# A hybrid decoder block on one core: filler products of both attentions in another order, the bias table written from another queue, four output tiles finished at full width

## The chip, the cores and the metric

The kernel runs on one core of one Trainium2 chip. A core has TensorE (PE: matmuls; its weight loads are shown as PEld), VectorE (DVE), ScalarE (ACT), GpSimd (POOL) and SyncE (SP, which here only issues DMAs). Each engine works through its own instructions in order and waits for the others by semaphores. DMAs are issued from an engine's queue; in this kernel SP issues nearly all of them. The metric is the device time of one execution in microseconds (us), as a median over runs.

## The reference

One layer for 512 tokens of width 1024 and 256 memory tokens, all in float32. Two kinds of heads read the same normed x; then come cross-attention and an MLP:

```python
h = rms_norm(x, norm_mix[l])
qa, ka, va, qg, kg, vg, glr, rg = jnp.split(h @ w_in[l], offsets, axis=-1)
o_a = moba_attention(qa, ka, va, rp_table)
log_a = jax.nn.log_sigmoid(glr @ w_gate_up[l] + b_gate[l]) / G_GATE_NORM
o_g = gla_chunked(qg, kg, vg, log_a)
o_g = rms_norm(o_g, g_norm[l]).reshape(B, T, G_WIDTH) * jax.nn.silu(rg)
x = x + jnp.concatenate([o_a, o_g], axis=-1) @ w_out[l]
...
return rms_norm(x, norm_final)
```

`o_a` has 8 heads of 64, causal, with a bias by relative position; `o_g` has 4 heads. Left out are cross-attention (xq, kx, vx, xo) and the MLP with its squared ReLU, each added to x. With two blocks of 256 tokens the block-sparse attention sees all earlier tokens, so it is causal softmax attention with a bias by distance.

## The kernel before

**Precision and products.** Each float32 operand is split into two float16 parts, high and low, by an ACT copy and a DVE subtraction (`split`, L276 to L278; for weights L115 and L116, into tiles whl). A product is three matmuls: high by high, high by low, low by high. `gemm_steps` (L225) gives one such step of three matmuls for each 128 rows of the contraction; a tile of 512 tokens takes 8 steps, 24 matmuls of 512 columns.

**Order on PE.** PE's order is the order in which the code is written; the other engines' instructions are put in order by a scheduler, and a wait on one of them holds all that stands behind it there. To keep PE busy while another engine prepares the next thing, the code has a list of fillers (`Fill`, L252): generators of product steps, of which `fill(n)` runs the next n, `fill.until(k)` runs until k generators are left and `fill.drain()` runs all. Which product is in the list where (L744 to L746, L895, L907) and the numbers of the calls set PE's order.

**GLA stage (L744 to L787).** `Gla(pr)` makes the gates of two of the four heads: product z, then on ACT Abs, Exp, Ln (tile e) and on DVE two scans. `prep_fine` makes qF and kF (ACT exponents L577, L578; DVE L579, L580), which `small` multiplies into psL (L610); `prep_level` makes qz and kz, whose tiles POOL sets to zero (L590, L591), for the next products into psL. Fillers here are vg (values of the GLA heads), qk(0) and qk(1) (queries and keys of head pairs 0 and 1), and the memory's keys and values xk and xv.

**Memory squares.** `mem_steps` (L474) loads the memory tokens, splits them and sums their squares: four ACT squares (sqm), added on POOL into accm (L487, L491). The tiles sqm have two buffers, one of which was bvec's.

**Bias table.** bvec (8 heads by 384 distances) goes to DRAM as bscr1 (L724), and from there 128 times, each copy one element further, into the table bscr (L727): 1024 rows. Both writes are issued from ACT's queue. `load_bias` (L735) reads a pair's bias from it through SP and spreads one column on POOL (bq, L741).

**Attention stage (L895 to L921).** For each pair of heads i, `score` runs four query tiles (3, 2, 1, 0): s = q k (L810), maximum, exponent and sum, then P in two parts (pq, L838, L839). `trans` transposes P by DMA (L845), `attn_out` multiplies it by v (o, L857). A score needs the pair's qks, the split result of qk(i): eviction (L415), ACT split (L277), DVE split (L278). Fillers are va, qk(2), rg(1), qk(3), rg(2), rg(3); rg is the gate of the GLA output, with a chain of its own on ACT and DVE (L527 to L542) that ends in a part of mix, the input of the output projection.

**Output projection (L863 to L941).** Four of its eight tiles (NPRE) are begun early, over the parts of mix that are there (`early_steps`). `residual_steps` then finishes tile by tile for one half of the tokens (256), adds x (xr, L883) and sums the squares (`SumSq`: ACT L316, POOL L326, L327). While PE works on the second half, `normed` computes the first half's norm: total on PE (L332), ACT L284 to L286, DVE L287 and L289 (wout), then eight times a product (ynout, L299) and a split into act2, which the first xq products read.

Of the kernel before, what the change touches and what calls it, by code (L numbers as in the profile page):

```python
# [39 lines left out]
def hybrid_block_kernel(  # L40
# [163 lines left out]
    for n in range(8):  # L204
        W.add(("xv", n), w_xv[n])
    W.add(("tt", 8), w_tt[8])
    for n in range(4):
        W.add(("va", n), w_vv[n])
    for n in (2, 6, 9, 3, 7, 10, 11):
        W.add(("tt", n), w_tt[n])  # L210
    for nm, ap in (("out", w_out), ("xq", w_xq), ("xo", w_xo)):
        for n in range(8):
# [261 lines left out]
    def mem_steps():  # L474
        memf = [p1.tile([P, 2, M], F32, tag="va", bufs=4, name=f"memf{j}") for j in range(4)]
        accm = pst.tile([P, 512], F32, tag="acc", bufs=1, name="accm")
        for j in range(4):
            nc.sync.dma_start(memf[j], mem_t[:, 2 * j:2 * j + 2, :])
        for j in range(4):
            mf = memf[j].rearrange("p n t -> p (n t)")  # L480
            for k in (2 * j, 2 * j + 1):
                mk = memf[j][:, k % 2, :]
                ACT.activation(actm[k][:, 0, :], mk, AF.Copy, scale=gmem[:, k:k + 1])
                DVE.scalar_tensor_tensor(actm[k][:, 1, :], mk, gmem[:, k:k + 1], actm[k][:, 0, :], op0=ALU.mult, op1=ALU.subtract)
            if j == 0:
                ACT.activation(accm, mf, AF.Square)
                POOL.tensor_scalar(accm, accm, 512 * EPS / P, None, op0=ALU.add)  # L487
            else:
                sq = pst.tile([P, 512], F32, tag="sq", bufs=2, name=f"sqm{j}")
                ACT.activation(sq, mf, AF.Square)  # L490
                POOL.tensor_tensor(accm, accm, sq, op=ALU.add)  # L491
            yield from ()
        mem_acc.append(accm)

    mem_acc = []

# [48 lines left out]
    class Gla:  # L545
# [175 lines left out]
    bvec = pst.tile([P, 512], F32, tag="sq", bufs=2, name="bvec")[0:8, :NDIST]  # L721
    DVE.tensor_copy(bvec, psb[0:8, 0:NDIST])
    bscr1 = pdr.tile([8, NDIST], F32, name="bscr1")
    nc.scalar.dma_start(bscr1, bvec)  # L724
    bscr = pdr.tile([8, P, T], F32, name="bscr")

    nc.scalar.dma_start(  # L727
        bass.AP(tensor=bscr.tensor, offset=bscr.offset, ap=[[P * T, 8], [T + 1, P], [1, NDIST]]),
        bass.AP(tensor=bscr1.tensor, offset=bscr1.offset, ap=[[NDIST, 8], [0, P], [1, NDIST]]),
    )  # L730
# [10 lines left out]
            POOL.tensor_copy(bq[:, :256], bq[:, 256:257].to_broadcast([P, 256]))  # L741
            bias[p].append(bq)

    fill.add(*[vg_steps(t) for t in range(4)], qk_steps(0), mem_steps(), qk_steps(1), memsum_steps())  # L744
    fill.add(xk_steps(0), xk_steps(1), memrow_steps(), *[xk_steps(n) for n in range(2, 8)])
    fill.add(*[xv_steps(c, t) for c in range(2) for t in range(2)])  # L746
    gl = []
    for pr in range(2):
        fill(8 if pr == 0 else 4)
        gl.append(Gla(pr))  # L750
        if pr == 0:
            pw_ = sbank("wxt")
            for t in range(4):
                PE.transpose(pw_[:, t * P:t * P + P], wx[:, t * P:t * P + P], ident)
            DVE.tensor_scalar(wxt, pw_.rearrange("p (n t) -> p n t", t=P)[:, :, 0], SA * IX, None, op0=ALU.mult)
    for pr in range(2):
        if pr == 1:
            load_bias(0)
        G = gl[pr]
        a = G.prep_fine()  # L760
        fill(20 if pr == 0 else 6)
        G.banks()
        G.small(0, a)
        for i, s in enumerate((8, 16)):
# [107 lines left out]

    def residual_steps(nm, act, hf, ssq):
        c0 = hf * HT
        for n in range(8):
            if nm == "out" and n < NPRE:
                ps = early[n][:, c0:c0 + HT]
                yield from gemm_steps(ps, (nm, n), act, c0, c0 + HT, (2, 3), start=False, skip_group_check=True)
            else:
                ps = gbank(f"{nm}{n}_{hf}")[:, :HT]  # L880
                yield from gemm_steps(ps, (nm, n), act, c0, c0 + HT)
            xs = xr[n][:, c0:c0 + HT]
            DVE.scalar_tensor_tensor(xs, ps, IS, xs, op0=ALU.mult, op1=ALU.add)  # L883
            ssq.add(xs)

    xr = [None] * 8

# [527 lines left out]
```

## Time and profile before

| what | value |
| --- | --- |
| median of three runs | 715.57 us (715.09 to 715.87) |
| the profiled execution | 715.83 us, span 714.0 us |
| mean granted clock of TensorE | 0.983 |
| PE busy | 682.5 us, 96% of the span |
| DVE busy | 551.7 us, 77% |
| ACT busy | 417.0 us, 58% |
| POOL busy | 73.6 us, 10% |

The span is the time from the first to the last instruction in one profiled execution; the execution took 1.8 us more. In a timeline, a bracket such as `[6.79 <-DVE kF L580]` is the time that the engine had stood idle before that instruction, and the instruction that ended the wait. [...] `SPq` and `ACTq` are instructions that issue DMAs.

### The profile page before, as it was taken

How to read it: one execution, taken by the hardware profiler on the slowest of the kernel's cores; microseconds unless marked ns; L12 is line 12 of the kernel's file. 1: busy time of each engine (PE TensorE's matmuls, PEld its weight loads, DVE VectorE, ACT ScalarE, POOL GpSimd, SP SyncE). 2: the span in 40 equal slices, each digit the busy share in tenths (PEclk: the TensorE clock that was granted, in tenths of full speed). 3: DMA queues.
4: the chain of work that ended last, by engine and by line, in shares of the span. 5: the costliest groups of instructions: out<-in, count | busy, mean ns of one | idle time of the engine just before them, and what ended most of it. 6: DMA issues, size and time to landing. Idle time of an engine off the chain costs nothing.

```text
span 714.0 us, 13411 instructions
## 1 busy us (share of the span) xinstructions
PE 682.5 (96%) x5352; PEld 469.4 (66%) x5352; DVE 551.7 (77%) x987; ACT 417.0 (58%) x800; POOL 73.6 (10%) x90
## 2 busy tenths in 40 slices
PE   8996999999898997999999999999999999999995
PEld 3443486544343486888888854468888866488884
DVE  6957969768986638656639899889878889999825
ACT  8646465668775436355536666545444766665533
POOL 4013000000000044000124100000000000003211
PEclk9998999999998999899999999999999999999999
DMA  8860643443826604236404231203343352314003
GB/s 310 277 231 16 211 142 118 163 151 66 258 90 171 185 1 148 89 62 176 105 16 143 95 118 60 88 31 120 118 129 110 123 167 64 118 54 136 20 1 119
DMA packets 57059, 85.68 MB, mean 120 GB/s; under 512 B 32123, under 2 KB 37540, under 8 KB 56996
## 3 DMA queue, kind: packets, MB, share of 16 engines
q1 hardware_dynamic: 55948, 83.24, 37.2%
q10 hardware_dynamic: 1048, 1.59, 0.6%
q8 instruction: 42, 0.69, 0.4%
q14 instruction: 21, 0.17, 0.1%
HBM read 75.36 MB, written 3.68 MB: 111 GB/s over the span
## 4 chain that ended last, share of the span: by engine, by line
PE 56%; DVE 7%; ACT 3%; issue 2%; POOL 1%; DVEq 0%; ACTq 0%; POOLq 0%
PE up L233 6%; PE up L231 6%; PE up L232 6%; PE a L1186 4%; PE a L1187 4%; PE a L1188 4%; PE xq L232 2%; PE xq L233 2%; PE xq L231 2%; PE c L1187 2%; PE c L1186 2%; PE c L1188 2%; DVE whl L116 1%; PE xo L233 1%; PE xo L232 1%
## 5 line engine op out<-in xcount | busy, mean ns | idle before, releaser
L116 DVE SCALAR_TENSOR_TENSOR whl<-wst,whl 128x1024 f16<-128x1024 f32 (+1 forms) x165 | 195.5, 1191 | 27.1 <-ACT whl L115 26.5
L115 ACT ACTIVATE whl<-wst 128x1024 f16<-128x1024 f32 (+1 forms) x165 | 166.2, 1014 | 44.0 <-PE a L1188 7.8
L233 PEld LDWEIGHTS <-whl 128*128 128x128 f16 x744 | 73.5, 99 | 44.0 <-issue 6.1
L231 PEld LDWEIGHTS <-whl 128*128 128x128 f16 x744 | 73.4, 99 | 39.8 <-issue 4.5
L232 PEld LDWEIGHTS <-whl 128*128 128x128 f16 x744 | 73.4, 99 | 38.4 <-issue 3.8
L231 PE MATMUL up<-act,whl 128*128 128x512 f16 (+1 forms) x224 | 78.1, 349 | 0.0
L232 PE MATMUL up<-act,whl 128*128 128x512 f16 (+1 forms) x224 | 78.1, 349 | 0.0
L233 PE MATMUL up<-act,whl 128*128 128x512 f16 (+1 forms) x224 | 78.1, 349 | 0.0
L1186 PE MATMUL a<-t,whl 128*128 128x256 f16 x192 | 52.3, 273 | 1.1 <-ACT v L1203 1.1
L1187 PE MATMUL a<-t,whl 128*128 128x256 f16 x192 | 52.3, 273 | 0.0
L1188 PE MATMUL a<-t,whl 128*128 128x256 f16 x192 | 52.3, 273 | 0.0
L1187 PEld LDWEIGHTS <-whl 128*128 128x128 f16 x456 | 44.6, 98 | 6.9 <-issue 1.5
L1186 PEld LDWEIGHTS <-whl 128*128 128x128 f16 x456 | 44.6, 98 | 5.2
L1188 PEld LDWEIGHTS <-whl 128*128 128x128 f16 x456 | 44.6, 98 | 4.9
L232 PE MATMUL xq<-act,whl 128*128 128x256 f16 x128 | 36.0, 281 | 3.3 <-DVE act L278 3.3
L231 PE MATMUL xq<-act,whl 128*128 128x256 f16 x128 | 35.9, 281 | 0.9 <-ACT act L277 0.9
L233 PE MATMUL xq<-act,whl 128*128 128x256 f16 x128 | 36.0, 281 | 0.0
L233 PE MATMUL xo<-ox,whl 128*128 128x256 f16 x128 | 34.9, 273 | 0.0
L232 PE MATMUL xo<-ox,whl 128*128 128x256 f16 x128 | 34.9, 273 | 0.0
L231 PE MATMUL xo<-ox,whl 128*128 128x256 f16 x128 | 34.9, 273 | 0.0
L277 ACT ACTIVATE t<-hs 128x512 f16<-128x512 f32 x32 | 19.8, 624 | 23.9 <-DVE hs L1068 23.8
L232 PE MATMUL out<-mix,whl 128*128 128x256 f16 (+1 forms) x104 | 30.9, 297 | 0.1
(334 smaller groups left out, 1642.8 us busy)
## 6 DMA issues: line engine op xcount, KB each, us to landing
wst<-in_w_up SPq DMA_DIRECT2D x32, 512.0 KB, 3.6
wst<-in_w_down SPq DMA_DIRECT2D x32, 512.0 KB, 3.7
wst<-in_w_tt SPq DMA_DIRECT2D x12, 512.0 KB, 4.6
wst<-in_w_vv SPq DMA_DIRECT2D x8, 512.0 KB, 3.5
wst<-in_w_xk SPq DMA_DIRECT2D x8, 512.0 KB, 5.7
wst<-in_w_xv SPq DMA_DIRECT2D x8, 512.0 KB, 3.5
wst<-in_w_out SPq DMA_DIRECT2D x8, 512.0 KB, 4.8
wst<-in_w_xq SPq DMA_DIRECT2D x8, 512.0 KB, 3.6
```

The lines of the kernel that those rows point to most:

```text
L115: ACT.activation(wt[:, 0, c], stg[:, c], AF.Copy, scale=SW)
L116: DVE.scalar_tensor_tensor(wt[:, 1, c], stg[:, c], SW, wt[:, 0, c], op0=ALU.mult, op1=ALU.subtract)
L231: PE.matmul(ps, wt[:, 0, kt, :], a[:, 0, c0:c1], start=st, stop=False, **kw)
L232: PE.matmul(ps, wt[:, 0, kt, :], a[:, 1, c0:c1], start=False, stop=False, **kw)
L233: PE.matmul(ps, wt[:, 1, kt, :], a[:, 0, c0:c1], start=False, stop=sp, **kw)
L277: ACT.activation(dst_h, src, AF.Copy, scale=scale)
L1186: PE.matmul(ps, w[:, 0, kt, :], b[:, 0, c], start=st, stop=False, skip_group_check=not start)
L1187: PE.matmul(ps, w[:, 0, kt, :], b[:, 1, c], start=False, stop=False, skip_group_check=not start)
L1188: PE.matmul(ps, w[:, 1, kt, :], b[:, 0, c], start=False, stop=sp, skip_group_check=not start)
```

## The change

It has four parts.

- **GLA stage.** Both `Gla` objects are made at one place, after seven filler steps; the steps after the first `prep_fine` are 25 instead of 20, those after the second 8 instead of 6. `mem_steps` now runs inside `qk_steps(1)`, one of its four pieces every four steps.
- **Bias table.** Both writes are issued from POOL's queue.
- **Attention stage.** The fillers stand in the order qk(2), va, qk(3), rg(1), rg(2), rg(3), with the weights in a matching order, and the counts between scores and the places of `attn_out` change.
- **Output projection.** The four early tiles are finished for all 512 tokens within the first half; the second half has the other four tiles alone.

```diff
-    for n in (2, 6, 9, 3, 7, 10, 11):
+    for n in (3, 7, 9, 10, 11):
...
-        for j in range(4):
+        for j, _ in enumerate(qk_steps(1)):
+            yield
+            if j % 4 or j > 12:
+                continue
+            j //= 4
             mf = memf[j].rearrange("p n t -> p (n t)")
...
-    nc.scalar.dma_start(bscr1, bvec)
+    nc.gpsimd.dma_start(bscr1, bvec)
...
-    nc.scalar.dma_start(
+    nc.gpsimd.dma_start(
         bass.AP(tensor=bscr.tensor, offset=bscr.offset, ap=[[P * T, 8], [T + 1, P], [1, NDIST]]),
...
-    fill.add(*[vg_steps(t) for t in range(4)], qk_steps(0), mem_steps(), qk_steps(1), memsum_steps())
+    fill.add(*[vg_steps(t) for t in range(4)], qk_steps(0), mem_steps(), memsum_steps())
...
-        fill(8 if pr == 0 else 4)
-        gl.append(Gla(pr))
...
+    fill(7)
+    gl = [Gla(0), Gla(1)]
...
-        fill(20 if pr == 0 else 6)
+        fill(25 if pr == 0 else 8)
...
+        if nm == "out":
+            ns = range(NPRE, 8)
+            if hf == 0:
+                for n in range(NPRE):
+                    yield from gemm_steps(early[n], (nm, n), act, 0, T, (2, 3), start=False, skip_group_check=True)
+                    DVE.scalar_tensor_tensor(xr[n], early[n], IS, xr[n], op0=ALU.mult, op1=ALU.add)
+                    for i in range(2):
+                        ssq[i].add(xr[n][:, i * HT:i * HT + HT])
...
-    fill.add(*[va_steps(t) for t in range(4)], qk_steps(2), rg_steps(1), qk_steps(3), rg_steps(2), rg_steps(3))
+    fill.add(qk_steps(2), *[va_steps(t) for t in range(4)], qk_steps(3), *[rg_steps(h) for h in (1, 2, 3)])
...
-            fill.until({2: 4, 3: 2}[i])
+            fill.until({2: 4, 3: 3}[i])
...
-                fill(5 if i < 3 else 3)
+                fill((5, 6, 5, 3)[i])
...
-            if 1 <= i < 4 and g == 3:
-                fill.until(5)
-                attn_out(pairs.pop(i - 1))
+        if 1 <= i < 4:
+            if i == 1:
+                fill.until(4)
+            fill((0, 4, 0, 4)[i])
+            attn_out(pairs.pop(i - 1))
         if i < 4:
             pairs[i].trans()
-            fill(4)
+            fill((4, 0, 0, 0)[i])
```

What stands in a row on the engines that wait, at three places. First POOL from the memory's first square on, before:

```order
L487 TENSOR_SCALAR accm_807<-accm_807 128x512
L741 COPY bq0_1191<-bq0_1191 128x256
L741 COPY bq1_1194<-bq1_1194 128x256
L491 TENSOR_TENSOR accm_807<-accm_807,sqm1_822 128x512
L491 TENSOR_TENSOR accm_807<-accm_807,sqm2_829 128x512
L491 TENSOR_TENSOR accm_807<-accm_807,sqm3_836 128x512
L590 MEMSET qz8_0_629 128x32x8
L591 MEMSET kz8_0_630 128x32x8
```

and after:

```order
L730 DMA bscr1_413<-bvec_411 8x384
L493 TENSOR_SCALAR accm_807<-accm_807 128x512
L733 DMA bscr_415<-bscr1_413 8x128x384
L596 MEMSET qz8_0_629 128x32x8
L597 MEMSET kz8_0_630 128x32x8
L596 MEMSET qz16_0_686 128x16x16
L597 MEMSET kz16_0_687 128x16x16
L497 TENSOR_TENSOR accm_807<-accm_807,sqm1_881 128x512
L497 TENSOR_TENSOR accm_807<-accm_807,sqm2_911 128x512
L497 TENSOR_TENSOR accm_807<-accm_807,sqm3_936 128x512
L747 COPY bq0_1191<-bq0_1191 128x256
L747 COPY bq1_1194<-bq1_1194 128x256
```

The adds into accm have moved from behind the two bias copies to ahead of them, and the two table writes and the memsets of qz and kz stand ahead of both.

Second, DVE at the first score of pair 3, before (L814 ISA is the score's addition of bias with its maximum, p3_3_0 the first of pair 3; qkf7 and qks7 are pair 3's keys; whl is a weight split):

```order
L415 SCALAR_TENSOR_TENSOR qkf7_2409<-qk7_2347,wx_124 128x512
L116 SCALAR_TENSOR_TENSOR whl48_2815<-wst48_2814,whl48_2815 128x1024
L278 SCALAR_TENSOR_TENSOR qks7_2408<-qkf7_2409,qks7_2408 128x512
L814 ISA p3_3_0_2431,sm4_3_2422<-s3_3_0_2423,bq6_2171 128x512
L814 ISA sm4_3_2422 128x1
L814 ISA p3_3_1_2433,sm4_3_2422<-s3_3_1_2424,bq7_2174 128x512
```

and after, DVE at the eviction of pair 3's keys, which stands further ahead, at pair 2's last score tile (p2_0_0) and behind the pieces of pair 2's tiles 3 and 2 (pq2):

```order
L842 SCALAR_TENSOR_TENSOR pq2_0_2261<-p2_2_0_2252,sm4_2_2196,pq2_0_2261 128x3x128
L842 SCALAR_TENSOR_TENSOR pq2_1_2262<-p2_2_1_2254,sm4_2_2196,pq2_1_2262 128x3x128
L818 TENSOR_SCALAR sm4_2_2196<-sm4_2_2196 128x2
L417 SCALAR_TENSOR_TENSOR qkf7_2309<-qk7_2232,wx_124 128x512
L817 ISA p2_0_0_2339,sm4_2_2196<-s2_0_0_2331,bq4_1965 128x128
```

The keys' eviction now stands ahead of pair 2's last score tile. DVE at pair 3's scores after the change (rgsq1, rgnw1 belong to rg(1); p3_2 is pair 3's second score tile):

```order
L544 SCALAR_TENSOR_TENSOR rgsq1_2369<-rgsq1_2369,rgnw1_2370 128x512
L818 TENSOR_SCALAR sm4_3_2422<-sm4_3_2422 128x2
L817 ISA p3_2_0_2455,sm4_3_2422<-s3_2_0_2447,bq6_2197 128x384
L817 ISA sm4_3_2422 128x1
L545 SCALAR_TENSOR_TENSOR rgnw1_2370<-rgsq1_2369,rgnw1_2370 128x512
L817 ISA p3_2_1_2457,sm4_3_2422<-s3_2_1_2448,bq7_2200 128x384
```

rg(1)'s chain, which ended before pair 3's keys, runs between pair 3's scores.

Third, DVE at the norm behind the output projection, before (xr is the addition to x, wout0 the norm's factor of the first half, ynout0_0 the first normed tile):

```order
L883 SCALAR_TENSOR_TENSOR xr3_2625<-out3_2689,xr3_2625 128x256
L116 SCALAR_TENSOR_TENSOR whl52_3164<-wst52_3163,whl52_3164 128x1024
L116 SCALAR_TENSOR_TENSOR whl53_3196<-wst53_3195,whl53_3196 128x1024
L883 SCALAR_TENSOR_TENSOR xr4_2627<-out4_1_2990,xr4_2627 128x256
L287 SCALAR_TENSOR_TENSOR wout0_3107<-ssqout0_2981,wout0_3107 128x256
L116 SCALAR_TENSOR_TENSOR whl54_3230<-wst54_3229,whl54_3230 128x1024
L289 SCALAR_TENSOR_TENSOR wout0_3107<-wout0_3107,yout0_3106 128x256
L116 SCALAR_TENSOR_TENSOR whl55_3262<-wst55_3261,whl55_3262 128x1024
L883 SCALAR_TENSOR_TENSOR xr5_2629<-out5_1_3019,xr5_2629 128x256
L299 SCALAR_TENSOR_TENSOR ynout0_0_3113<-xr0_2619,gneg_87,wout0_3107 128x256
```

and after:

```order
L891 SCALAR_TENSOR_TENSOR xr4_2627<-out4_1_2960,xr4_2627 128x256
L116 SCALAR_TENSOR_TENSOR whl55_3234<-wst55_3233,whl55_3234 128x1024
L289 SCALAR_TENSOR_TENSOR wout0_3079<-ssqout0_2982,wout0_3079 128x256
L291 SCALAR_TENSOR_TENSOR wout0_3079<-wout0_3079,yout0_3078 128x256
L891 SCALAR_TENSOR_TENSOR xr5_2629<-out5_1_2991,xr5_2629 128x256
L301 SCALAR_TENSOR_TENSOR ynout0_0_3085<-xr0_2619,gneg_87,wout0_3079 128x256
L301 SCALAR_TENSOR_TENSOR ynout0_1_3089<-xr1_2621,gneg_87,wout0_3079 128x256
L301 SCALAR_TENSOR_TENSOR ynout0_2_3093<-xr2_2623,gneg_87,wout0_3079 128x256
L280 SCALAR_TENSOR_TENSOR act2_0_2748<-ynout0_0_3085,act2_0_2748 128x256
```

Two of the four weight splits ahead of ynout0_0 stood between the parts of the norm's chain; in the new piece one stands ahead of wout0, and none between it and ynout0_0.

## Rows read from the trace of the kernel before

**Rows 1.** Page, parts 1 (busy) and 5 (count, busy us, mean ns, idle).
```profile
PE 682.5 (96%) x5352; PEld 469.4 (66%) x5352; DVE 551.7 (77%) x987; ACT 417.0 (58%) x800; POOL 73.6 (10%) x90
...
L116 DVE SCALAR_TENSOR_TENSOR whl<-wst,whl 128x1024 f16<-128x1024 f32 (+1 forms) x165 | 195.5, 1191 | 27.1 <-ACT whl L115 26.5
```

**Rows 2.** Windows at the table's write and place 1; the first row names columns.
```profile
core 0: us, PE busy (x) PEld busy (x) DVE busy (x) ACT busy (x) POOL busy (x), PEclk, DMA share, GB/s
40.00:54.40 14.40, 14.40 (x67) 6.49 (x65) 6.53 (x11) 6.56 (x13) 0.07 (x1) 1.00 0.48 170
61.50:65.40 3.90, 3.84 (x72) 1.86 (x73) 3.90 (x8) 3.88 (x8) 0.56 (x2) 0.50 0.00 0
```

**Rows 3.** PE's timeline, first GLA products: start us, us, operation, idle before.
```profile
54.39 0.38 PE L248 MATMUL vg<-whl,act 128*128 128x512 f16 x1
...
61.56 0.89 PE L610 MATMUL psL<-qF,kF 64*32 64x32 f32 x64 [6.79 <-DVE kF L580]
...
111.55 0.75 PE L610 MATMUL psL<-qF,kF 64*32 64x32 f32 x64 [1.38 <-DVE kF L580]
```

**Rows 4.** Timelines of ACT, SP and POOL, 38 to 59 us.
```profile
38.99 0.73 ACTq L727 DMA_DIRECT2D bscr<-bscr  x1
...
53.65 0.81 SPq L740 DMA_DIRECT2D bq<-bscr  x2
...
55.85 0.84 POOL L741 COPY bq<-bq 128x256 f32<-128x256 f32 x2 [15.78 <-DMA bq<-bscr]
56.66 4.30 POOL L491 TENSOR_TENSOR accm<-accm,sqm 128x512 f32<-128x512 f32 x3
...
57.95 0.63 ACT L490 ACTIVATE sqm<-memf 128x512 f32<-128x512 f32 x1 [4.61 <-POOL accm L491]
```

**Rows 5.** PE's timeline at the first scores of pairs 2 and 3.
```profile
192.28 0.39 PE L810 MATMUL s<-qks,qks 64*128 64x512 f16 x2 [1.69 <-ACT qks L277]
193.35 0.61 PE L810 MATMUL s<-qks,qks 64*128 64x512 f16 x4 [0.68 <-DVE qks L278]
...
215.75 0.61 PE L810 MATMUL s<-qks,qks 64*128 64x512 f16 x2 [2.67 <-ACT qks L277]
216.83 1.03 PE L810 MATMUL s<-qks,qks 64*128 64x512 f16 x4 [0.47 <-DVE qks L278]
```

**Rows 6.** Windows from pair 3's first score to o(3), columns as in rows 2.
```profile
217.20:222.60 5.40, 5.40 (x19) 1.47 (x15) 1.48 (x5) 1.52 (x4) 0.00 (x0) 0.51 0.94 245
222.60:238.50 15.90, 15.90 (x99) 7.33 (x98) 13.14 (x40) 12.41 (x30) 0.00 (x0) 1.00 0.50 167
238.50:245.20 6.70, 6.63 (x32) 2.75 (x31) 5.00 (x8) 1.98 (x3) 0.00 (x0) 1.00 1.06 237
```

**Rows 7.** DVE's timeline, end of rg(1), pair 2's last pieces.
```profile
211.16 0.68 DVE L278 SCALAR_TENSOR_TENSOR mix<-rgx,mix 128x512 f16<-128x512 f32 x1
...
213.04 1.40 DVE L839 SCALAR_TENSOR_TENSOR pq<-p,sm,pq 128x256 f16<-128x256 f32 x4
```

**Rows 8.** DVE's and PE's timeline at o(3).
```profile
243.93 0.69 DVE L278 SCALAR_TENSOR_TENSOR mix<-rgx,mix 128x512 f16<-128x512 f32 x1 [0.69 <-ACT mix L277]
...
245.20 1.82 PE L857 MATMUL o<-pT,vas 128*64 128x512 f16 x24
```

**Rows 9.** Timelines of PE, ACT and DVE along the norm behind the out projection.
```profile
266.24 0.60 PE L332 MATMUL ssqout<-accout,ones 128*128 128x256 f32 x2
...
269.69 0.42 ACT L316 ACTIVATE sqout<-xr 128x256 f32<-128x256 f32 x1 [1.54 <-POOL accout L327]
...
276.67 1.74 DVE L299 SCALAR_TENSOR_TENSOR ynout<-xr,gneg,wout 128x256 f32<-128x256 f32 x3
...
284.60 0.75 DVE L278 SCALAR_TENSOR_TENSOR act<-ynout,act 128x256 f16<-128x256 f32 x2
```

**Rows 10.** Windows at the first xq product, columns as in rows 2.
```profile
277.60:285.00 7.40, 3.25 (x20) 1.82 (x19) 7.40 (x17) 5.36 (x11) 3.15 (x3) 0.92 0.27 80
285.00:290.60 5.60, 5.54 (x25) 3.88 (x25) 3.04 (x5) 0.60 (x2) 2.06 (x1) 0.50 0.71 221
```

More of the change, by code (lines that the diff above doesn't have):

```diff
@@ L206, in hybrid_block_kernel @@
     W.add(("tt", 8), w_tt[8])
+    for n in (2, 6):
+        W.add(("tt", n), w_tt[n])
     for n in range(4):
         W.add(("va", n), w_vv[n])
-    for n in (2, 6, 9, 3, 7, 10, 11):
+    for n in (3, 7, 9, 10, 11):
         W.add(("tt", n), w_tt[n])
@@ L491, in mem_steps @@
                 POOL.tensor_tensor(accm, accm, sq, op=ALU.add)
-            yield from ()
-        mem_acc.append(accm)
+            if j == 3:
+                mem_acc.append(accm)
     mem_acc = []
@@ L742, in load_bias @@
             bias[p].append(bq)
-    fill.add(*[vg_steps(t) for t in range(4)], qk_steps(0), mem_steps(), qk_steps(1), memsum_steps())
+    fill.add(*[vg_steps(t) for t in range(4)], qk_steps(0), mem_steps(), memsum_steps())
     fill.add(xk_steps(0), xk_steps(1), memrow_steps(), *[xk_steps(n) for n in range(2, 8)])
     fill.add(*[xv_steps(c, t) for c in range(2) for t in range(2)])
-    gl = []
-    for pr in range(2):
-        fill(8 if pr == 0 else 4)
-        gl.append(Gla(pr))
[L751 to L755, printed above, removed]
+    fill(7)
+    gl = [Gla(0), Gla(1)]
+    pw_ = sbank("wxt")
+    for t in range(4):
+        PE.transpose(pw_[:, t * P:t * P + P], wx[:, t * P:t * P + P], ident)
+    DVE.tensor_scalar(wxt, pw_.rearrange("p (n t) -> p n t", t=P)[:, :, 0], SA * IX, None, op0=ALU.mult)
     for pr in range(2):
@@ L874, in residual_steps @@
         c0 = hf * HT
[L875 to L881, printed above, removed]
+        ns = range(8)
+        if nm == "out":
[6 more added lines that the diff above has]
+                        ssq[i].add(xr[n][:, i * HT:i * HT + HT])
+        for n in ns:
+            ps = gbank(f"{nm}{n}_{hf}")[:, :HT]
+            yield from gemm_steps(ps, (nm, n), act, c0, c0 + HT)
             xs = xr[n][:, c0:c0 + HT]
             DVE.scalar_tensor_tensor(xs, ps, IS, xs, op0=ALU.mult, op1=ALU.add)
-            ssq.add(xs)
+            ssq[hf].add(xs)
     xr = [None] * 8
@@ L906, in hybrid_block_kernel @@
             load_xr()
-            fill.add(early_steps(), residual_steps("out", mix, 0, ssq[0]))
+            fill.add(early_steps(), residual_steps("out", mix, 0, ssq))
         for g in range(4):
@@ L936, in hybrid_block_kernel @@
     fill.drain()
-    fill.add(residual_steps("out", mix, 1, ssq[1]))
+    fill.add(residual_steps("out", mix, 1, ssq))
     fill(7)
@@ L1026, in hybrid_block_kernel @@
     ssq = sums("xo", *HALVES)
-    fill.add(residual_steps("xo", ox, 0, ssq[0]))
+    fill.add(residual_steps("xo", ox, 0, ssq))
     xattn(1)
     fill.drain()
-    fill.add(residual_steps("xo", ox, 1, ssq[1]))
+    fill.add(residual_steps("xo", ox, 1, ssq))
     fill(7)
```

## The prediction

> **What bounds the kernel.** The page comes first: PE is busy 682.5 of 714.0 us, DVE 551.7, ACT 417.0 [rows 1]. So the time is TensorE's stream, and only two things can shorten it: fewer matmul columns, or less time in which PE waits or runs at its lower clock. The change takes 24 weight loads and 24 matmuls away but no columns: 48 products of 256 columns become 24 of 512. [...] What is left is PE's idle time. I went along PE's own timeline for idle brackets, and through windows around them for the granted clock. Five places hold nearly all of it:
>
> 1. First GLA product. PE starts the last matmul of its vg tile at 54.39 and psL at 61.56 [rows 3]: 7.0 lost. [...] Together 8.5.
> 2. The same product of the second GLA pair: 1.38 idle at 111.55 [rows 3].
> 3. Pair 2's first score: 1.69 + 0.68 idle [rows 5], 2.4, at full clock.
> 4. Pair 3's first score: 2.67 + 0.47 idle [rows 5], 3.1, and then 5.4 us at clock 0.51 [rows 6], which costs half of them, 2.6: 5.7.
> 5. The first xq product, behind the out projection: 20 matmuls of 256 columns in 7.4 us, where 2.2 would do, and then 5.54 us busy at clock 0.50 [rows 10]: 5.2 + 2.8 = 8.0.
>
> Together 26.0 us.
>
> **Place 1: the table and the memory squares.** The chain is read backwards. psL waits for DVE's kF [rows 3], that for ACT's exponents, and those stand in ACT's queue behind a square (L490) at 57.95 that waited 4.61 us for POOL's accm. POOL began these three adds (4.30 us) only at 56.66, behind two bq copies at 55.85, for whose data it had sat 15.78 us [rows 4]. bq is read from the table that ACT's queue writes at 38.99. After the change POOL does the adds first and the copies last, and mem's squares are spread over qk_steps(1), ahead of their use. That takes the wait off this chain. What replaces it: ACT's square of the third piece now waits until POOL's small write, bscr1, has landed, since it takes bvec's buffer, and Gla(0)'s Abs, Exp and Ln and the two exponents of qF and kF are queued behind it on ACT. In before the same landing was over by 38.99, when ACT's second write went out. Counting from there with Gla's operations at 0.4 to 0.7 us each, two scans at 1.2, and the vg copy and a whl split among them (1.19 [rows 1]), I estimate kF at 51.5. PE needs it at 54.5, so there are 3 us of slack; below that the cost is nothing, above it 1 for 1. Moving z by three matmuls costs 0.1 at most. Gain 8.4.
>
> The two POOL writes have no row: no DMA goes out on POOL in before. The nearest rows are ACT's: the large write took 0.73 us to issue, which is the lower bound. For the upper one I let POOL be held from there until SP's bq loads go, 39.7 to 53.65, 13.9 us [rows 4]. Queued behind the write are four memsets, and the first user of these is the second psL product, at 54.5 + 0.7 + 12 x 0.213 = 57.8. Neither end reaches PE. I take no cost, being nearest to the 0.73; from 57.8 on it is 1 for 1. On SP the bq loads wait for the table with weight loads behind them; they now stand behind ten weight tiles instead of five, so the tiles that PE needs next are ahead of them.
>
> Where that write goes out DVE is busy 6.53 of 14.40 us [rows 2]. [...]
>
> **Place 2.** fill(8) for fill(6) puts two more steps, six matmuls of 512 columns or as many of 256 twice over, 1.3 us, ahead of the second psL. Gain 1.3.
>
> **Places 3 and 4: the scores.** qk(2) now stands before the va products and qk(3) before rg(1): pair 2's keys are finished 32 steps ahead of its first score and pair 3's eight, where there was one step. Eight steps are 24 x 0.213 = 5.1 us, against the 3.1 that PE waited for the eviction and the splits [rows 5]. Both losses go: 2.4 + 5.7 = 8.1.
>
> What is late next is the tail of pair 3. rg(1) used to be through DVE by 211.16 [rows 7], before pair 3's scores. Now its seven DVE operations (up to 0.68 each, 4.8) fall among them, with pair 2's last four pieces (1.40) and o(1)'s split (0.69): 6.9 us more. From 217.2 to 245.2 DVE is busy 1.48 + 13.14 + 5.00 = 19.6 of 28.0 us [rows 6]; of its 8.4 idle, 2.6 were PE's half clock and go, 5.8 stay. The tail has little slack: the last mix was split from 243.93 for 0.69, so to 244.6, and o(3) goes at 245.20 [rows 8]; pair 3's transposes land at about the same time. 6.9 into 5.8 is 1.1 over if every gap can be filled, and 0 if the stall's end helps ACT as much; 3.2 if three waits of DVE for ACT like the 0.69 at 243.93 [rows 8] stay; 8 if all of it and a split of 1.19 land behind the last product. I take 3.5, nearest to the wait that is a row. Idleness of 3.1 was followed by the half clock at place 4, of 2.4 was not at place 3, so I add 1.5, about half of a stretch like place 4's. 5.0 lost at o(3); attention nets 3.1.
>
> **Place 5: out.** Four out tiles are finished at full width in the first half, so its second half has 32 steps, not 40. From the total of the squares (266.24 [rows 9], after seven of these steps) to xq there are 25 steps x 3 x 0.107 = 8.0 us where there were 10.6: 2.6 less cover. Against it, the chain from that total to the first ynout took until 276.67, 10.4 us; of that 1.54 was ACT's wait for POOL [rows 9], and three whl splits of 1.19 [rows 1] stood in DVE's way. In the new order the slots of out0 to out3 come free 2.6 us earlier and their followers' splits go ahead: one split stands before wout and none between it and the first ynout, where there were two on either side; the squares of the four full tiles are added long before. 10.4 - 1.5 - 3.6 = 5.3. The eight pairs of ynout and act then took 276.67 to 284.60 + 0.75, 8.7 [rows 9]; with one split fewer among them about 7.9. So the last act stands 13.2 after the total, and PE wants it at 8.0 + 7 x 0.321 = 10.3. 2.9 us of idleness remain, in pieces, so I count no half clock. Gain 8.0 - 2.9 = 5.1. Bounds: all hidden, 8.0; only the cover lost, -2.6.
>
> **The sum.** 8.4 + 1.3 + 3.1 + 5.1 = 17.9. From the first xq product on the order is the same. The profiled execution took 715.83 (span 714.0 and 1.8 around it), 0.26 above the median of 715.57: 715.83 - 17.9 - 0.26 = 697.7. I forecast **697.5 us**, rounded.
>
> **Rivals.**
> - A: pair 3's tail fits, and the norm's last act comes in time. DVE's gaps before 222.6 are waits for PE at half clock, which speaks for it. 697.5 - 5.0 = 692.5, with the norm hidden too 689.6.
> - B: the tail gives attention's gain back: 8 idle and 2.7 at half clock at o(3) for the 5.0. The little slack of before speaks for it. 703.2.
> - C: the norm chain keeps its length and only loses cover: 8.0 + 2.6 for 2.9. Against it, the splits do stand elsewhere in the order. 705.2.
> [...]
> - E, slower: POOL is held by the 1024 rows of the table write itself. PE loses 1 for 1 past 57.8; to lose 17.9 and 1.4 more it must be held to 77.1, 37.4 us for one write, 50 times ACT's issue. From there on the time is above 717.
> - F: the losses only move (place 1's to the second psL, 3 and 4's to o(2) and o(3), 5 as in C): near 715.5.
>
> **Chances.** Forecast 0.44, A 0.22, B 0.11, C 0.09, D 0.07, E 0.05, F 0.02. The range leaves out E, F and little besides: 690 to 706. Faster by over 0.2% (about what a measurement of this kernel can tell from no change): all but E and F, 0.93; within 0.2%: 0.02; slower: 0.05.
>
> **What will show it.** Right: no idle bracket over 1 us at psL near 54.5, POOL's adds ahead of its copies and its DMA issues short; none ahead of the first scores of pairs 2 and 3; one of 0 to 5 us near o(3), released by DVE's mix or the transposes; some 3 us of waits for act at xq, with clock 1.00 after. Wrong: PE waiting between 55 and 65 for a memset or for ACT's exponents (D, E), clock 0.50 after o(3) (B), waits of 5 us and more at xq (C).

## The result, and the profile after

The changed kernel took 707.69 us (706.36 to 710.12, four runs), the kernel before 715.72 (715.09 to 717.06): a ratio of 0.9889, 95% interval 0.9857 to 0.9921. On another chip, later, it was 0.9906 (0.9887 to 0.9925). So it is faster, by about 1% (0.8 to 1.4 and 0.8 to 1.1), and the forecast of 697.5 with 690 to 706 gave it more than twice what it got. The profiled execution took 706.36 us, with a span of 704.2: 9.8 less than before, where the sum had 17.9.

The page, part 1 (busy us, share, instructions); it answers to [rows 1]:

```profile
PE 677.6 (96%) x5328; PEld 465.6 (66%) x5328; DVE 554.8 (79%) x983; ACT 416.4 (59%) x800; POOL 80.7 (11%) x92
```

PE is 5 us less busy, mostly because fewer matmuls run at half clock (its mean granted clock is 0.992, where it was 0.983); ACT works as long as before, DVE 3.1 us and POOL 7.1 us longer. As before, the rest is to be read from PE's idle brackets. At the start of the GLA stage (PE's timeline, for [rows 3]):

```profile
55.56 0.76 PE L616 MATMUL psL<-qF,kF 64*32 64x32 f32 x64
...
58.64 0.38 PE L235 MATMUL qk<-act,whl 128*128 128x512 f16 x1
65.13 0.88 PE L616 MATMUL psL<-qz,kz 64*32 64x32 f32 x64 [6.11 <-DVE kz L604]
65.94 0.61 PE L233 MATMUL qk<-act,whl 128*128 128x512 f16 x1
66.34 0.63 PE L234 MATMUL qk<-act,whl 128*128 128x512 f16 x1
...
68.05 0.46 PE L235 MATMUL qk<-act,whl 128*128 128x512 f16 x1
```

The first product, at 55.56, waits for nothing any more. The second, at 65.13, waits 6.11 us for kz, and the products behind it start 0.43 us apart until 68.05, where those ahead of it start 0.22 apart. From 65.13 to 68.05 the window shows PEclk, the share of its full clock that TensorE was granted, at 0.50, as it was behind the first product in before [rows 2]. The loss of place 1 has moved by one product. DVE's timeline shows what kz waited for, and below it ACT's has kz's exponent:

```profile
52.05 0.42 DVE L603 TENSOR_TENSOR qz<-qz,gqk 128x256 f32<-128x256 f32 x1
...
55.68 1.23 DVE L570 TENSOR_TENSOR_SCAN g<-rmask,e 128x512 f32<-128x512 f32 x1
56.82 7.82 DVE L116 SCALAR_TENSOR_TENSOR whl<-wst,whl 128x1024 f16<-128x1024 f32 x4
64.57 0.41 DVE L604 TENSOR_TENSOR kz<-kz,gqk 128x256 f32<-128x256 f32 x1
```

```profile
57.98 0.41 ACT L602 ACTIVATE kz<-d 128x256 f32<-128x256 f32 x1
```

qz was multiplied at 52.05. kz's multiplication, its twin of 0.41 us, comes at 64.57: it stands in DVE's queue behind Gla(1)'s scans and four weight splits, and these four took 7.82 us. kz's exponent, its input, was through ACT at 58.39; a multiplication directly behind it would have been done at 58.8 (estimate: 58.39 and 0.41), when PE's last matmul, of 58.64, was running out. POOL's timeline in the same stretch, for [rows 4]:

```profile
40.56 1.20 POOL L733 DMA_DIRECT2D bscr<-bscr  x1
41.76 0.33 POOL L596 MEMSET qz<- 128x256 f32 x1
42.01 0.33 POOL L597 MEMSET kz<- 128x256 f32 x1
56.96 0.31 POOL L596 MEMSET qz<- 128x256 f32 x1 [14.63 <-DVE g L570]
...
57.50 6.06 POOL L497 TENSOR_TENSOR accm<-accm,sqm 128x512 f32<-128x512 f32 x3
70.81 1.73 POOL L747 COPY bq<-bq 128x256 f32<-128x256 f32 x2 [7.25 <-DMA bq<-bscr]
```

The large table write took POOL 1.20 us to issue, and the memsets of qz and kz that stand behind it were done by 42.4. They had been the prediction's worry, and nothing waited for them. Later in the GLA stage, PE's timeline at the second pair's product of z into psL (the mid product), and at pair 0's third score tile; neither waited in before:

```profile
123.53 0.46 PE L625 MATMUL psL<-z 64*32 64x32 f32 x32 [0.65 <-DVE z L604]
...
160.74 0.27 PE L813 MATMUL s<-qks,qks 64*128 64x256 f16 x1 [1.01 <-DVE sm L817]
162.01 0.50 PE L813 MATMUL s<-qks,qks 64*128 64x256 f16 x5 [1.00 <-DVE mix L716]
```

and ahead of o(3), for [rows 8]:

```profile
239.12 0.38 PE L233 MATMUL out<-mix,whl 128*128 128x512 f16 x1 [1.25 <-ACT mix L279]
239.85 0.38 PE L234 MATMUL out<-mix,whl 128*128 128x512 f16 x1 [0.35 <-DVE mix L280]
...
240.37 1.85 PE L860 MATMUL o<-pT,vas 128*64 128x512 f16 x24
```

Pairs 2 and 3 have no bracket at their first scores, so [rows 5] have no counterpart. The windows at the first xq product, for [rows 10], show 1.6 us of idleness at clock 1.00:

```profile
273.00:279.00 6.00, 4.40 (x39) 3.47 (x37) 6.00 (x12) 2.81 (x7) 3.19 (x2) 1.00 0.17 54
279.00:285.00 6.00, 6.00 (x56) 5.29 (x55) 4.91 (x13) 2.97 (x8) 0.00 (x0) 1.00 0.62 211
```

A wait of 0.79 is new further on, at the first output of cross-attention, for a transpose by DMA:

```profile
322.62 0.28 PE L1006 MATMUL xo<-xpT,vx 128*128 128x256 f16 x1 [0.79 <-DMA xpT<-xpq]
```

Place by place, in us (idle brackets, and what half clock cost behind them; start to start each wait is some 0.15 longer):

| place | lost before | forecast to be left | left |
| --- | --- | --- | --- |
| 1, first GLA pair | 8.5 | 0.1 | 6.1 + 1.1 = 7.2, at the second product |
| 2, second GLA pair | 1.4 | 0.1 | 0 at psL; 2.0 at pair 0's scores, 0.65 at the mid product |
| 3 and 4, scores; o(3) | 8.1 | 5.0 | 1.6 |
| 5, xq | 8.0 | 2.9 | 1.6 |
| cross-attention's first output | 0 | 0 | 0.8 |

26.0 had been lost, 8.1 were to be left, 13.9 are. That makes 12.1 gained, where the span gained 9.8. PE starts psL at 55.56 instead of 54.6, which takes 1.0 of the difference (0.4 lies in the kernel's first matmuls, 0.2 is a wait of the z products for glr); two more brackets than before, each some 0.15 short, take 0.3. About 1 us is not assigned.

### The profile page after: what moved, and what is told of

Its sections match the earlier page's. It is cut to its first block, busy times and chain, and to the rows that moved or that the text cites. A ratio compares the mean times of both kernels' runs of the same rounds, so it can differ in the third digit from the quotient of the medians.

```text
span 704.2 us, 13359 instructions
## 1 busy us (share of the span) xinstructions
PE 677.6 (96%) x5328; PEld 465.6 (66%) x5328; DVE 554.8 (79%) x983; ACT 416.4 (59%) x800; POOL 80.7 (11%) x92
## 4 chain that ended last, share of the span: by engine, by line
PE 74%; DVE 15%; ACT 4%; DMA 3%; issue 2%; POOL 1%; SPq 0%; DVEq 0%; ACTq 0%; POOLq 0%
PE up L234 6%; PE up L233 6%; PE up L235 6%; PE a L1196 4%; DVE whl L116 4%; PE a L1198 4%; PE a L1197 4%; PE g L407 2%; PE xq L234 2%; PE qk L233 2%; PE xq L235 2%; PE xq L233 2%; PE c L1198 2%; PE c L1196 2%; PE c L1197 2%
## 5 line engine op out<-in xcount | busy, mean ns | idle before, releaser
L116 DVE SCALAR_TENSOR_TENSOR whl<-wst,whl 128x1024 f16<-128x1024 f32 (+1 forms) x165 | 199.5, 1216 | 29.1 <-ACT whl L115 28.6
L115 ACT ACTIVATE whl<-wst 128x1024 f16<-128x1024 f32 (+1 forms) x165 | 166.4, 1014 | 52.1 <-PE qk L235 10.3
L235 PEld LDWEIGHTS <-whl 128*128 128x128 f16 x736 | 72.1, 98 | 41.0 <-issue 2.3
L233 PEld LDWEIGHTS <-whl 128*128 128x128 f16 x736 | 72.1, 98 | 40.0 <-issue 4.1
L234 PEld LDWEIGHTS <-whl 128*128 128x128 f16 x736 | 72.1, 98 | 39.0 <-issue 3.8
L1197 PEld LDWEIGHTS <-whl 128*128 128x128 f16 x456 | 44.6, 98 | 6.8 <-issue 1.5
L1196 PEld LDWEIGHTS <-whl 128*128 128x128 f16 x456 | 44.6, 98 | 5.2
L1198 PEld LDWEIGHTS <-whl 128*128 128x128 f16 x456 | 44.6, 98 | 5.0
L234 PE MATMUL xq<-act,whl 128*128 128x256 f16 x128 | 34.9, 272 | 0.8 <-DVE act L280 0.8
L233 PE MATMUL xq<-act,whl 128*128 128x256 f16 x128 | 34.9, 273 | 0.8 <-ACT act L279 0.8
L235 PE MATMUL xq<-act,whl 128*128 128x256 f16 x128 | 34.9, 273 | 0.0
L328 POOL TENSOR_SCALAR accf<-accf 128x128 f32<-128x128 f32 (+1 forms) x3 | 3.5, 1169 | 249.5 <-ACT accf L318 249.5
```

Of the source, the lines that this page charges most:

```text
L115: ACT.activation(wt[:, 0, c], stg[:, c], AF.Copy, scale=SW)
L116: DVE.scalar_tensor_tensor(wt[:, 1, c], stg[:, c], SW, wt[:, 0, c], op0=ALU.mult, op1=ALU.subtract)
L233: PE.matmul(ps, wt[:, 0, kt, :], a[:, 0, c0:c1], start=st, stop=False, **kw)
L234: PE.matmul(ps, wt[:, 0, kt, :], a[:, 1, c0:c1], start=False, stop=False, **kw)
L235: PE.matmul(ps, wt[:, 1, kt, :], a[:, 0, c0:c1], start=False, stop=sp, **kw)
L328: POOL.tensor_scalar(self.acc, self.acc, 1024 * EPS / P, None, op0=ALU.add)
```

## The experiments

Two theories stood. Q: place 1's loss came back because of the order on DVE, with the splits ahead of kz, and POOL's adds beside the splits make them longer (C, for contention, not the prediction's rival). P: POOL's writes themselves hold something up.

**The table back on ACT's queue.**

```diff
-    nc.gpsimd.dma_start(bscr1, bvec)
+    nc.scalar.dma_start(bscr1, bvec)
...
-    nc.gpsimd.dma_start(
+    nc.scalar.dma_start(
         bass.AP(tensor=bscr.tensor, ...
```

> The changed kernel with both table writes put back on ACT's queue, nothing else. Theory Q (order on DVE): in the changed kernel the second GLA product (psL of qz, kz) waits 6.1 us because kz's last multiplication stands on DVE behind four weight splits; POOL's queue matters only through the order that it brings. Here kz stands ahead of these splits again, but its memset stands on POOL behind the two bias copies and two adds, so psL should wait some 2 to 4 us there, released by kz, and the total should be 2 us faster to 3 us slower than the changed kernel, 705 to 710. Theory P (POOL's own writes cost the time: descriptors, or a late landing): the wait goes altogether and the time falls by 7 to 8, to about 700. If ACT's queue was what held place 1 in the kernel before, some 4 us or more of idleness come back at the first psL.

Measured: 708.02 us (706.93 to 709.33), ratio 0.9896 (0.9870 to 0.9922): the changed kernel's time. PE's timeline:

```profile
58.39 0.76 PE L616 MATMUL psL<-qF,kF 64*32 64x32 f32 x64 [2.38 <-DVE kF L586]
...
65.30 0.89 PE L616 MATMUL psL<-qz,kz 64*32 64x32 f32 x64 [3.45 <-POOL kz L597]
```

POOL's timeline shows the old order, bias copies, two adds, and only then the memsets:

```profile
55.92 1.15 POOL L747 COPY bq<-bq 128x256 f32<-128x256 f32 x2 [14.95 <-DMA bq<-bscr]
57.04 7.70 POOL L497 TENSOR_TENSOR accm<-accm,sqm 128x512 f32<-128x512 f32 x2
64.69 0.31 POOL L596 MEMSET qz<- 128x256 f32 x1
64.94 0.30 POOL L597 MEMSET kz<- 128x256 f32 x1
```

So the queue changes what PE waits for (2.38 and 3.45 us instead of 6.11), not how long. The wait at the second product is released by POOL's kz, as Q had it, and its size was right. That the first product would wait too I had only as a remark. P's forecast of about 700 did not come: without POOL's writes nothing is won. Nor did they land late in the changed kernel: the large one was there 14.1 us after its issue, and in before SP's loads of the table could go 14.7 us after ACT's issue (38.99 and 53.65 [rows 4]). The two adds took 7.70 us here, beside a busy DVE; in before three took 4.30 [rows 4].

**POOL's adds made small.** Only 8 of 512 columns are added; the rest of the sum is left out.

```diff
-                POOL.tensor_tensor(accm, accm, sq, op=ALU.add)
+                POOL.tensor_tensor(accm[:, :8], accm[:, :8], sq[:, :8], op=ALU.add)
```

> The changed kernel, but POOL adds only 8 of the 512 columns of the memory's squares (three adds; the rest of the sum is left out), so that POOL is nearly idle while DVE splits weights; the order on DVE stays. Theory C (POOL's adds slow DVE down: four splits took 7.82 us beside them instead of 4.8): the splits take 1.2 us each, kz is ready about 3 us earlier, psL waits about 3 us instead of 6.1, PE may keep its full clock behind it, and the time falls by 3 to 4.5, to 702 to 704. If the two engines don't slow each other, the splits stay at 1.95 us and the time at 706 to 707.5.

Measured: 704.01 us (702.41 to 704.90), ratio 0.9841 (0.9820 to 0.9862). DVE's timeline:

```profile
57.76 4.62 DVE L116 SCALAR_TENSOR_TENSOR whl<-wst,whl 128x1024 f16<-128x1024 f32 x4
62.31 0.41 DVE L604 TENSOR_TENSOR kz<-kz,gqk 128x256 f32<-128x256 f32 x1
```

The splits by themselves (duration in ns, least, median, most), first in the changed kernel and then here:

```profile
L116 DVE SCALAR_TENSOR_TENSOR whl<-wst,whl x4: 1202/2279/2302, 56.8 to 62.4; 128x1024 f16<-128x1024 f32 x4
```

```profile
L116 DVE SCALAR_TENSOR_TENSOR whl<-wst,whl x4: 1198/1216/1223, 57.8 to 61.2; 128x1024 f16<-128x1024 f32 x4
```

Beside POOL's adds a split takes 2.28 us, without them 1.22; four took 7.82 and take 4.62. PE's wait at the second psL fell from 6.11 to 3.08, and the ratio from 0.9889 to 0.9841. The half clock stayed (0.53 from 63.5 to 66.9, where the products start 0.43 us apart). C holds: in the changed kernel each of three splits takes 1.06 us more beside adds of 1.66, 2.12 and 2.12 us, where an add in before took 1.27 (median of three).

**The memsets of qz and kz on DVE.** This takes them off POOL's queue, behind the write.

```diff
-                POOL.memset(v3(qz, 2 * s)[:, :, :s], 0.0)
+                (POOL if self.pr else DVE).memset(v3(qz, 2 * s)[:, :, :s], 0.0)
...
```

> The changed kernel with the first pair's four memsets of qz and kz on DVE instead of POOL, behind the table write no more. This makes the order on DVE put kz directly behind qz, ahead of the weight splits. Theory Q: the wait at the second psL falls from 6.1 to under 1.5 us and the half clock behind it goes; time 698 to 701. Theory P: the wait stays or moves on to the next thing that POOL's write delays; 705 to 708.

Measured: 713.16 us (711.18 to 714.62), ratio 0.9965 (0.9947 to 0.9984): a miss. PE's timeline:

```profile
37.13 1.98 PE L559 MATMUL z<-glr,csb 128*128 128x512 f32 x4 [0.91 <-DVE glr L417]
...
65.60 0.76 PE L616 MATMUL psL<-qz,kz 64*32 64x32 f32 x64 [3.10 <-DVE kz L604]
...
89.22 1.22 PE L506 MATMUL ssm<-accm,ones 128*128 128x256 f32 x2 [4.88 <-POOL accm L497]
```

The wait at the second product is gone, as Q had it, since kz now follows qz on DVE. But the next pair of tiles, of the third product, has its kz behind splits again and costs 3.10 (with clock 1.00 behind it, from 65.8 to 69), and mem's last square slid so far back on ACT that the sum of the squares waits 4.88 for POOL. Taking one instruction out of the row lets the scheduler put the rest in another order: a loss cured at one wait comes back at the next. Q's reason was right, its sum was not.

**Attention and output alone**, without the GLA start and without POOL's queue.

```diff
-    fill(7)
-    gl = [Gla(0), Gla(1)]
+    gl = []
+    for pr in range(2):
+        fill(8 if pr == 0 else 4)
+        gl.append(Gla(pr))
...
-    nc.gpsimd.dma_start(bscr1, bvec)
+    nc.scalar.dma_start(bscr1, bvec)
```

(The fills of 25 and 8 and mem's place in the row are those of before, too.)

> The kernel before with the attention order and the output tiles of the change, but without the GLA start and without POOL's queue for the table. If places 1 and 2 net nothing in the changed kernel (8.5 and 1.4 lost before; 6.3 and 1.2 at the second psL, 2.3 at pair 0's scores and 0.8 at the other pair's mid product lost after), this takes 706 to 708.5, like the changed kernel. If the GLA start and the queue do bring the 8 us that the prediction gave them, it takes 714 or more, since then attention and output bring next to nothing.

Measured: 704.92 us (703.33 to 705.81), ratio 0.9854 (0.9833 to 0.9875). This is below what was expected, by a little, and faster than the whole change: the other two parts do not net nothing, they cost some 3 us (0.9854 beside 0.9889 and 0.9906; only the first two intervals overlap). PE's timeline has the first psL's loss of before, and no wait at pair 0's scores:

```profile
62.44 0.89 PE L612 MATMUL psL<-qF,kF 64*32 64x32 f32 x64 [6.96 <-DVE kF L582]
```

**POOL's queue alone on top of that**, with the GLA start of the kernel before. Against the last kernel:

```diff
-    nc.scalar.dma_start(bscr1, bvec)
+    nc.gpsimd.dma_start(bscr1, bvec)
...
```

> Attention order, output tiles and POOL's queue for the table on the GLA start of the kernel before. With POOL's queue the order on DVE has the four weight splits ahead of kz also without the early second Gla. Theory Q: the first psL waits under 1.5 us, the second 5 to 7 with the half clock behind it, so the time is 705 to 707.5, no faster than without POOL's queue (704.9). If the early second Gla is needed for the wait (its scans stand ahead of kz too), the second psL waits under 3 us and the time is 699 to 702.

Measured: 705.55 us (704.74 to 706.38), ratio 0.9869 (0.9853 to 0.9884). DVE's and PE's timelines:

```profile
57.07 7.81 DVE L116 SCALAR_TENSOR_TENSOR whl<-wst,whl 128x1024 f16<-128x1024 f32 x4
64.80 0.41 DVE L600 TENSOR_TENSOR kz<-kz,gqk 128x256 f32<-128x256 f32 x1
```

```profile
65.36 0.88 PE L612 MATMUL psL<-qz,kz 64*32 64x32 f32 x64 [7.38 <-DVE kz L600]
```

The four splits and kz stand here as in the changed kernel, and PE waits 7.38. So it is the move to POOL's queue that brings the splits ahead of kz, with or without the early second Gla: the program's order on DVE changes with a DMA on another engine. Why the scheduler orders so, no run shows. With the first experiment (table on ACT's queue) this makes a square: neither part 0.9854, the queue alone 0.9869, the GLA start (with its two extra fillers) alone 0.9896, both 0.9889 and 0.9906. Neither part gains anything, in any company.

**The changed kernel once more**, beside the kernels with parts of it, for this comparison.

> The changed kernel itself, on the chip of the two others, for comparison: 706.4 to 710, with 6.1 us of waiting at the second psL, 2.2 at pair 0's scores, about 1.6 ahead of o(3).

Measured: 707.81 us (707.49 to 709.89), ratio 0.9906 (0.9887 to 0.9925).

**Six fillers instead of eight** ahead of the second pair's first product.

```diff
-        fill(25 if pr == 0 else 8)
+        fill(25 if pr == 0 else 6)
```

> The changed kernel with 6 instead of 8 fillers ahead of the second pair's first product, as in the kernel before. In the changed kernel pair 0's scores lost 2.3 us (1.2 and 1.2 at the third tile), which the kernel with attention and output alone did not. Theory: the two fillers are taken from the end of the GLA stage, where DVE's norm and rg(0) chains needed them as cover. So pair 0's loss falls to under 0.5 and 1.4 comes back at the second pair's psL: 705.5 to 707.5, 0 to 2 us faster than the changed kernel. If pair 0's loss comes from the earlier bias copies or the order of rg(0), it stays and the time is 708.5 to 709.5.

Measured: 706.51 us (704.85 to 707.65), ratio 0.9859 (0.9819 to 0.9900). The two waits at pair 0's scores and the one at the mid product are gone, and PE's timeline has the old one back:

```profile
112.18 0.75 PE L616 MATMUL psL<-qF,kF 64*32 64x32 f32 x64 [1.38 <-DVE kF L586]
```

The two fillers had saved 1.38 us there and cost 2.0 and 0.65 later. The brackets show this; the times alone do not, since the interval overlaps those of the changed kernel.

**Attention alone, and output alone.** The other parts are those of before; the core of each, against the kernel before:

```diff
...
-    fill.add(*[va_steps(t) for t in range(4)], qk_steps(2), rg_steps(1), qk_steps(3), rg_steps(2), rg_steps(3))
+    fill.add(qk_steps(2), *[va_steps(t) for t in range(4)], qk_steps(3), *[rg_steps(h) for h in (1, 2, 3)])
...
```

```diff
...
+                    yield from gemm_steps(early[n], (nm, n), act, 0, T, (2, 3), start=False, skip_group_check=True)
...
```

> The kernel before with the attention order alone. By the traces the stalls of pairs 2 and 3 (2.7 and 3.7 us and some 2 at half clock) go and 2 to 2.5 us come at the last product ahead of o(3): 708.5 to 710. By the prediction (3.1 net) it is 711.5 to 712.5. If the idleness only moves to xq or to the norm, 714 or more.

Measured: 710.28 us (709.61 to 710.60), ratio 0.9915 (0.9885 to 0.9945), some 6 us faster than before: the traces' figure, not the prediction's.

> The kernel before with the output tiles of the change alone. The prediction gave this part 5.1 us (7.9 lost at xq before, 2.9 after), which puts it at 710 to 711.5. In the kernels with attention and output together xq lost 1.9 us and had its full clock, so 6.0 would be gained there, less about 1 at the first cross-attention output, which waits for a transpose by DMA there and does not in the kernel before: 709.5 to 711. Rival: the 2.6 us of lost cover come back at xq without the attention order ahead of it: 714 or more.

Measured: 711.60 us (711.30 to 711.82), ratio 0.9953 (0.9936 to 0.9969): 3.6 gained, less than both expectations. At xq PE has its full clock, 1.00; this is the window there:

```profile
277.00:283.00 6.00, 4.39 (x38) 3.46 (x36) 6.00 (x13) 3.76 (x9) 2.72 (x2) 1.00 0.02 5
```

1.6 us of idleness, as in the changed kernel, so 6.4 are gained at the place itself. Of the rest, 1.6 (start to start) went to the new wait at the first cross-attention output, and the first GLA product happened to lose 0.8 more than in the other trace. In the runs of both together (0.9854) the gains of the two parts (0.85% and 0.47%) add up.

**The adds on DVE.** If the loss of place 1 is POOL's adds, behind the copies or beside the splits, they can be taken off POOL.

```diff
-                POOL.tensor_tensor(accm, accm, sq, op=ALU.add)
+                DVE.tensor_tensor(accm, accm, sq, op=ALU.add)
```

First on attention and output with the GLA start of before:

> Attention order and output tiles of the change on the GLA start of the kernel before, table on ACT's queue, but the three adds of the memory's squares on DVE instead of POOL (so POOL has the two bias copies and then the memsets). Beside the kernel with attention and output alone (704.9), whose first psL lost 7.1 us. Theory Q: that loss is ACT's square waiting for POOL's adds behind the bias copies; without it kF is ready near 55, the first psL waits 0 to 2.5 us, the splits stay behind kz, and the time is 697 to 700. If the late vg copies and Ln on ACT or the second table write hold the chain by themselves, 4 us or more stay and the time is above 701.

Measured: 699.08 us (697.33 to 699.89), ratio 0.9754 (0.9714 to 0.9794), the fastest of all. PE's timeline at the first product:

```profile
56.20 0.76 PE L612 MATMUL psL<-qF,kF 64*32 64x32 f32 x64 [1.30 <-DVE kF L582]
```

1.30 instead of 6.96, and behind it the products start 0.22 us apart, as at full clock, where they started 0.43 apart behind the 6.96. Then with the GLA start of the change and six fillers:

> All of the change but POOL's queue and the two extra fillers of the second pair (6, as before, instead of 8), and the three adds on DVE. Both Gla objects stand early, kz stands ahead of the weight splits, and nothing of ACT waits for POOL. Theory Q: the first psL waits under 1 us, the second under 1.5, pair 0's scores lose nothing; 695.5 to 699, the fastest of all. If the early second Gla costs by itself (its scans and exponents ahead of the first pair's), it is not faster than the kernel with the GLA start of before and the adds on DVE.

Measured: 701.52 us (700.71 to 702.23), ratio 0.9788 (0.9743 to 0.9834). A miss: 2.4 us slower than the last kernel, on the same chip and with no overlap of the runs. So the GLA start costs something by itself; whether it is the early second Gla or the squares inside `qk_steps(1)`, this run does not separate:

```profile
37.83 1.98 PE L559 MATMUL z<-glr,csb 128*128 128x512 f32 x4 [0.81 <-DVE glr L417]
...
58.81 0.76 PE L616 MATMUL psL<-qF,kF 64*32 64x32 f32 x64 [2.38 <-DVE kF L586]
...
63.73 0.76 PE L616 MATMUL psL<-qz,kz 64*32 64x32 f32 x64 [1.47 <-POOL kz L597]
```

The two z products, moved three matmuls ahead, wait 0.81 for glr; the first psL waits 2.38, later than with the old start, since kF is later here.

## Why the prediction was wrong

**The direction** was right, and so was the reading of what bounds the kernel: five stalls of PE, at the rows named. The size was not.

**Place 1 (8.4 forecast, about 1.3 got) is the step that failed.** For the first product the chain was read right: the adds behind the bias copies held ACT, and with them gone from it psL's first product starts on time; kF stood at 52.1 (estimate: 51.5). What failed is the path to the second product. The prediction followed it through POOL's queue alone, to the four memsets behind the write, and as neither bound of the write's price reached PE, it took no cost. For POOL that was right: the write took 1.20 us, near the lower bound. But the second product also needs kz's multiplication on DVE. DVE's order ahead of it was in no term, and so stood at nothing without a reason. The runs show 6.11 us of wait there, in two halves. One is the order, four splits directly ahead of kz: at 1.19 each [rows 1] they would have cost 4.8 us of DVE, some 3 of PE's wait, and the 3.08 measured without POOL's adds is that price. The other 3 us are contention: the adds no longer ran while DVE mostly waited, but beside these splits. A hint stood in DVE's timeline of before, where kF took 1.76 us beside the third add and qF, the same operation, 0.69:

```profile
59.13 0.69 DVE L579 TENSOR_TENSOR qF<-qF,gqk 128x512 f32<-128x512 f32 x1 [4.53 <-ACT qF L577]
59.74 1.76 DVE L580 TENSOR_TENSOR kF<-kF,gqk 128x512 f32<-128x512 f32 x1
```

Of the 8.5 that this place lost, 7.0 are the idleness and 1.5 the half clock behind it, 0.50 from 61.5 to 65.4 [rows 2]. And no run shows the 0.213 and 0.107 us that the sums, here and at places 2, 3 and 5, take for a matmul of 512 and of 256 columns: in the trace of before they start 0.216 and 0.109 us apart at full clock (medians), and those of 512 columns 0.427 at half clock. For the cover at xq that is 8.2 us instead of 8.0 (estimate: 75 times 0.109). Two matmuls of 256 columns take about what one of 512 takes, so the wider out products of the change gain nothing by themselves, and the sum counts nothing for them.

**The rivals and the signs.** E priced POOL's write too high: it was over at 41.76, and no stall came from it. What D rested on no run shows: the write took 1.20 us here, and the same 1.20 beside a busy DVE (POOL's queue on the GLA start of before). F was the right kind, "place 1's to the second psL", but was given 0.02 as a case in which everything moves (its own terms add up to some 716.7, not 715.5); it should have stood for place 1 by itself. The signs named for "right" came, if not in size, but the one at psL looked at the first product alone, and for a wait between 55 and 65 only memsets and ACT's exponents were named as what would end it.

**Place 2 (1.3 forecast, -1.3 got).** Fillers are not made, they are moved. The prediction counted the two steps where they were put and had no term for where they would be missing; the kernel with six fillers shows that end to be worth 2.65 us of brackets (2.0 at pair 0's scores, 0.65 at the mid product), more than the 1.38 that were saved.

**Places 3 and 4 (3.1 net forecast, 6.5 got).** Both stalls went, as forecast. The tail's mechanism was right, PE waits for the last mix, but 1.6 and not 3.5, and no half clock followed (1.00 from 240 to 246): in the 28 us before o(3) DVE was busy 25.8 us, 6.2 more than the 19.6 of before, where the sum let it take 5.8. The value lies between the bounds of 0 and 3.2, and the 1.5 added for half clock did not come. That is in part luck: with 1.71 and 0.35 us of waits there (table back on ACT's queue) and with 1.81 and 0.35 (attention and output with the adds on DVE) the clock did fall, to 0.54 and 0.56 for some 4 us (o(3)'s 24 matmuls took 3.27 and 3.03 us, where they took 1.85 in the changed kernel). The kernel with attention alone, some 6 us faster than its own before, confirms the gain.

**Place 5 (5.1 forecast, 6.4 got at xq).** The lost cover did not matter, since the chain got shorter by more, as forecast; 1.6 of idleness were left, not 2.9. But "from the first xq product on the order is the same" did not mean that nothing happens there: 0.8 to 1.6 went to a transpose.

In sum: 7.1 too much at place 1, 2.6 at place 2, about 1 each at the first xo and at the start; 3.4 too little at places 3 and 4, 1.3 at place 5. That is some 7 of the 8.1 us between the sum of 17.9 and the span's 9.8.

## What to carry to other kernels

When a wait is removed, follow the next consumer through every queue that feeds it, not only through the one that was edited; the order that a scheduler makes can put ready, unhurried work (weight splits) ahead of it on an engine that the diff doesn't touch. A filler that is spent at one stall is missing at the end of its stage: price that end. And do the cheap cure on its own first: attention, output and three adds on another engine took 0.9754 of the time of before, the whole change 0.9889 and 0.9906.

## What the runs showed of the hardware

- DVE and POOL slowed each other: a weight split of 128x1024 took 2.28 us instead of 1.22 beside POOL's adds of 128x512, and the adds took up to 2.12 instead of 1.27. POOL can lose far more: with the table back on ACT's queue two such adds took 7.70 us (from 57.04), while DVE's TENSOR_TENSOR operations of 128x512, back to back with others until 60.8, kept their 0.68 us.
- A DMA issued from POOL's queue held POOL 0.78 us (8 rows) and 1.20 us (1024 rows) in every kernel that had it so, where ACT's issue of the large one took 0.73 [rows 4]. In the changed kernel the large issue fell mostly into a gap of DVE (busy 0.35 of these 1.20 us); in the kernel with POOL's queue on the GLA start of before it ran beside a busy DVE and took the same 1.20 (POOL's and DVE's timelines):

```profile
40.18 1.20 POOL L729 DMA_DIRECT2D bscr<-bscr  x1
```

```profile
39.51 2.84 DVE L486 SCALAR_TENSOR_TENSOR mix<-memf,gmem,mix 128x256 f16<-128x256 f32 x7
```

- TensorE's idleness of 6.1 us was followed by the half clock (0.50), as were the 7.0 and 3.1 of before (0.50 and 0.51 [rows 2, 6]), the 4.88 (0.50 from 89.3 to 93), the 3.45 (products of 512 columns 0.43 us apart) and the 3.08 (0.53) of three experiments. A wait of 3.10 (the memsets on DVE) was not: the clock was 1.00 from 65.8 to 69. Two waits of 1.81 and 0.35 us were followed by clock 0.56 in one kernel, with 3.03 us for o(3); two of 1.86 and 0.35 were not in another (1.00, with 1.87 us for o(3)). So the length of the idleness alone does not tell, and no run here shows what else does.
- What stays open is why the changed kernel's runs lie up to 3.8 us apart. The spans of its two traces are 704.2 and 705.4 us, and the mean granted clock is 0.992 in both.
